# Two projections of values: 512 weight columns for four chunks of tokens in four PSUM banks, in place of 256 columns chunk by chunk

## The chip, the cores and the metric

The kernel runs on one core of one Trainium2 chip. The metric is the time of one execution on the device in microseconds (us), as the median of several runs. The profile shows one such execution.

## The reference

Two transformer blocks follow each other on 512 tokens of 1024 features. Each begins with a normalised and modulated input `u` and one wide projection of it, whose columns are then split into queries, keys, values and more:

```
z = u @ w_in[layer]
q_a, ..., q_b, k_b, v_b, m_a, m_b = jnp.split(z, split_at, axis=-1)          # first block
y_a = nsa_attention(q_a, ...) @ w_up_nsa;  y_b = stick_breaking_attention(q_b, k_b, v_b) @ w_up_sb
...
proj = hn @ w_in[l]
q_m, k_m, v_m, o_m, gates, q_a, k_a, v_a = jnp.split(proj, split_at, axis=-1)  # second block
h_m = mlstm_chunkwise(q_m, k_m, v_m, ...);  h_a = moba_attention(q_a, k_a, v_a)
```

The change touches how `v_b` of the first block and `v_a` of the second are computed. Both are a product of `u` (512 tokens by 1024) and 1024 by 512 weights.

## The kernel before, in words

Every fp32 product is made of three TensorE matmuls on operands split into a coarse and a fine part (`mm3`, L125, lines L127 to L129). `u` is held split, features on the partitions, as two tiles of 8 feature blocks by 512 tokens. Weights are loaded by `load` (L90) into one of two tiles `raw` of 1 MB, and split by `parts` (L104, L117: the coarse part on ACT, the fine part on DVE, 1024 columns at a time) into one of three pairs of tiles `w`.

Queries and keys are projected with the weights stationary and the 512 tokens moving (`project`, L816): each group of 128 output columns takes 24 matmuls of 512 columns, and PE's rows read `G<-u,w`. Values are wanted the other way round, tokens on the partitions. There `u` is stationary and the weights move (`project_rows`, L850): for each half of 256 columns it loads the weights, splits them in two calls, and goes through the four chunks of 128 tokens. A chunk takes 24 matmuls of 256 columns into one bank, and is copied out. PE's rows read `G<-w,u` with 128x256.

PSUM has eight banks. `ps` (L139) hands them out by tag: two banks `G`, three `S`, two `T`, one `O`. The banks of a tag go round in the order in which the program asks for them.

The order of instructions on each engine is set by a scheduler, which places work of later statements between that of earlier ones as far as data, banks and tiles allow. Two places matter here.

First block (`attention1`, L954): eight heads of one attention (`nsa_head`, L640) come first in the program. Their scores take the `S` banks (L679, L652), their transposes `T` (L522, L687), their output `O` (L691 once per head, as two matmuls; L530, L532). The projections of queries, keys and values of the other attention (L1024 to L1026, all in `G` banks) come behind the heads in the program. The scheduler lays their matmuls between the heads' on PE. So it does with the first groups of `take_m` (L1049), whose results can't leave their `G` banks before the heads end, since the tiles `mo` (L1042) lie where the heads' tiles lay. The heads of the second attention (`sb_head`, first matmul L743) start behind the last of the first eight.

Second block (`block2`, L1106): the projection of values (L1161) comes ahead of the eight heads `moba_head` (L1365, scores in `S` banks, L1383 and L1385). Two more projections, of 12 groups (L1165, L1166), and a third of values (L1167, `vm`, which stays on `project_rows`) are laid between these heads. Then come the four heads `mlstm_head` (L1299), each of which ends with a matmul L1353; the projection `mixa` (96 matmuls `G<-p,w`, L1188) is laid between them.

Of the kernel before, what the change touches and what calls it, by code (L numbers as in the profile page):

```python
# [14 lines left out]
AF = mybir.ActivationFunctionType  # L15
# [8 lines left out]
S, D = 512, 1024  # L24
# [48 lines left out]
class Kernel:  # L73
# [776 lines left out]
    def project_rows(self, u, name, c0, n, consume):  # L850

        for s in range(0, n, 256):
            w = self.load(self.w_cols(name, c0 + s, 256))
            w = [self.parts(w[:, 4 * i:4 * i + 4]) for i in range(2)]
            for t in range(4):
# [5 lines left out]
                if t % 2:  # L861
                    self.step()

    def block1(self, mods, dram, hp):


        nc = self.nc
        md = dram.tile([128, 16 * 512], F32, name="md")
        with ExitStack() as stack:
            with self.pool("b1n", "right") as wk:  # L870
                hr = wk.tile([128, 8, 512], F32, name="hr")
                with self.pool("b1a") as ap:
# [12 lines left out]
                    w = self.load(self.w_cols("w_in", 512, 256))  # L885
# [3 lines left out]
                u = [up.tile([128, 8, 512], F32R, name=f"u{i}") for i in range(2)]  # L889
# [64 lines left out]
    def attention1(self, u, md, first, dram):  # L954

        nc = self.nc
        kg = self.col("k_norm_g")
        gq = self.cp.tile([128, 1], F32, name="gq")
        nc.vector.tensor_scalar(gq, self.col("q_norm_g"), -0.125, None, op0=OP.mult)
        kd, vs = [], []  # L960
        sbq = self.sbq = ExitStack()
        with self.pool("nsap") as sp:

            places_a = Places([sbq.enter_context(self.pool("oa", "right"))] * 4, ("qn", "ob"), 1)
            qn = places_a.old[0]
            gates = sp.tile([128, 4, 4, 8], F32, name="gates")
            with self.pool("nsa0") as wk:

                def take_q(m, ps):
                    self.head_norm(ps, gq, qn[:, m], self.np)  # L970

                def take_k(b, ps):
                    kn = wk.tile([128, 512], F32, name="kn", bufs=2)
                    self.head_norm(ps, kg[:, b:b + 1], kn, wk)
                    t = [sp.tile([128, 2, 512], F32R, name=f"kd{b}{i}") for i in range(2)]
                    for g in range(2):
                        self.double(t[0][:, g], t[1][:, g], kn, 64 * g)
                    kd.append(t)

                def take_v(ps):  # L980
                    v = wk.tile([128, 512], F32, name="kn", bufs=2)
                    nc.scalar.activation(v, ps, AF.Copy)
                    t = sp.tile([128, 4, 2, 128], F32R, name=f"vs{len(vs)}")
                    self.values(t, v, wk)
                    vs.append(t)

                def take_kv(m, ps):
                    if m < 2:
                        self.compress_take(m, ps)
                    elif m in (2, 4):  # L990
                        take_k(m // 2, ps)
                    elif m in (3, 5):
                        take_v(ps)
                    else:
                        self.nsa_gates(ps, gates, wk)

                self.compress_start(wk)
                self.w_places = [(self.wp, 3)] * 3 + [(wk, 2)] * 2
                self.project(u, "w_in", 512, 896, take_kv, first=first, banks=[("G", 2)] * 2 + [("S", 3)] * 2)
                self.bias_bands(dram)  # L1000
                kdc, vsc = self.compress(sp, wk, kg[:, 0:1])
                self.project(u, "w_in", 0, 512, take_q)
                self.w_places = [(self.wp, 3)]

            sq = sbq.enter_context(self.pool("sbq", "right"))
            places = Places([sq] * 4, ("qT", "kT"))
            qT, kT = places.old
            vT = sq.tile([128, 4, 512], F32, name="vT")
            with self.pool("nsaw") as wk:

                heads = [self.nsa_head(h, qn, [[kd[b][i][:, h // 4] for i in range(2)] for b in range(2)], vs,
                                       kdc, vsc, gates, places_a.take, wk) for h in range(8)]
                self.in_turn(heads, 2)

            def keep(dst, scale):
                def f(m, ps):
                    nc.scalar.activation(dst[:, m], ps, AF.Copy, scale=scale)
                return f

            def take_vb(t, c0, ps):  # L1020
                nc.scalar.activation(vT[:, t, c0:c0 + 256], ps, AF.Copy)

            self.background = self.ada(0, [2, 3, 4])
            self.project(u, "w_in", 1304, 512, keep(qT, 0.125))  # L1024
            self.project(u, "w_in", 1816, 512, keep(kT, 1.0))
            self.project_rows(u, "w_in", 2328, 512, take_vb)  # L1026
        with self.pool("mo") as mw:
            self.sg = sbq.enter_context(self.pool("sg", "right"))
            with self.pool("sbw") as wk:

                self.in_turn([self.sb_head(h, qT, kT, vT, places.take, wk) for h in range(8)])


            self.kept = {}

            def take_m(first):
                def f(m, ps):
                    m += first
                    stay = m in (0, 1, 8)
                    t = self.sg.tile([128, 512], F32, name="sg", bufs=3) if stay else \  # L1040
                        mw.tile([128, 512], F32, name="mo", bufs=2)
                    nc.vector.tensor_copy(t, ps)  # L1042
                    if stay:
                        self.kept[m] = t
                    else:
                        nc.gpsimd.dma_start(md[:, m * 512:(m + 1) * 512], t)
                return f

            for m, n in ((2, 6), (10, 6), (0, 2), (8, 2)):  # L1049
                self.project(u, "w_in", 2840 + m * 128, n * 128, take_m(m))  # L1050
        return places_a.new, places.new
# [54 lines left out]
    def block2(self, h, u, up, mods, left, fp):  # L1106
# [8 lines left out]

        def rows_to(dst):
            def f(t, c0, ps):
                nc.vector.tensor_copy(dst[:, t, c0:c0 + 256], ps)
            return f

        vp = ExitStack()
        with up:
# [31 lines left out]
            with self.pool("vT", "right") as tp:  # L1154
                qT, kT = [Tiles([tp.tile([128, 1, 512], F32, name=f"{x}{j}") for j in range(4)], 1) for x in "qk"]
                vT = tp.tile([128, 4, 512], F32, name="vT")
                self.project(u, w_in, 2056, 512, keep(qT, -0.125), early=[None] * 3)
                with self.pool("mlr") as wk:
                    self.exps = [self.mlstm_rows(u, rows, acol, wk)]
                self.project(u, w_in, 2568, 512, keep(kT, 1.0))  # L1160
                self.project_rows(u, w_in, 3080, 512, rows_to(vT))  # L1161
                with self.pool("mbw") as wk:
                    for h8 in range(8):
                        self.moba_head(h8, qT, kT, vT, mixa, wk)
                    self.project(u, w_in, 1536, 512, keep(so, 0.5))  # L1165
                    self.project(u, w_in, 0, 1024, take_qk)  # L1166
                    self.project_rows(u, w_in, 1024, 512, rows_to(vm))  # L1167
# [797 lines left out]
```

## Time and profile before

| what | us |
|---|---|
| median of 3 runs (1805.99 to 1808.2) | 1807.76 |
| the profiled execution | 1805.68 |
| its span, first to last instruction | 1803.9 |
| TensorE (PE) busy | 1722.5 |
| VectorE (DVE) busy | 1397.3 |
| ScalarE (ACT) busy | 1143.0 |

Read the shares by stage, not as a whole. A busy PE is not a PE at its peak: matmuls are pipelined, a row lasts longer than the distance to the next one's start, and it is this distance that counts in a row of matmuls.

### The profile page before, as it was taken

Reading aid. Unit: us, or ns where it says so; the run is one execution under the profiler, and the core shown is the slowest. Engines: PE = TensorE matmul, PEld = TensorE weight load, DVE = VectorE, ACT = ScalarE, POOL = GpSimd, SP = SyncE. Lnnn points to the kernel's source line nnn. Section 1 sums busy time; section 2 is a strip of 40 time slices with the busy share of each in tenths; the row PEclk is TensorE's granted clock in tenths of the full one; section 3 lists DMA queues with packets and bytes.
Section 4 is the critical chain, followed back from the end, with each engine's and each line's share of the span. In section 5 each row is a group of like instructions: output and inputs, shape, how many; then the busy total and the mean of one; then the engine's idle time right before and its main releaser. Section 6 shows DMA issues by size and latency. Waiting matters only on the chain. (4 is left out here: it accounts for less than half of the span.)

```text
span 1803.9 us, 24830 instructions
## 1 busy us (share of the span) xinstructions
PE 1722.5 (95%) x8944; PEld 1414.6 (78%) x8944; DVE 1397.3 (77%) x2023; ACT 1143.0 (63%) x1805; POOL 474.6 (26%) x433
## 2 busy tenths in 40 slices
PE   5899999999999999999999999969999999999996
PEld 2678986787898888888979888757777777777775
DVE  4558888987788565657765867879999989999997
ACT  4356676665555343435555766558888878888886
POOL 2213424535133333333312410131212112121113
PEclk8999999999999999999999999979999999999998
DMA  8524213325655656564523215579999999999954
GB/s 324 166 92 129 83 59 116 102 87 164 197 180 165 208 182 201 177 207 149 165 71 94 63 56 175 212 232 345 356 360 362 348 313 385 376 365 364 371 204 168
DMA packets 233376, 377.71 MB, mean 209 GB/s; under 512 B 11817, under 2 KB 104613, under 8 KB 233248
## 3 DMA queue, kind: packets, MB, share of 16 engines
q1 hardware_dynamic: 221728, 345.60, 55.9%
q0 software_dynamic: 11520, 30.47, 5.5%
q8 instruction: 72, 1.18, 0.3%
q14 instruction: 56, 0.46, 0.1%
HBM read 366.64 MB, written 20.73 MB: 215 GB/s over the span
## 5 line engine op out<-in xcount | busy, mean ns | idle before, releaser
L117 ACT ACTIVATE w<-raw 128x1024 fp32r<-128x1024 f32 (+2 forms) x350 | 353.5, 1017 | 309.8 <-PE G L128 238.7
L117 DVE TENSOR_TENSOR w<-raw,w 128x1024 fp32r<-128x1024 f32 (+2 forms) x350 | 421.8, 1224 | 127.0 <-ACT w L117 123.6
L127 PE MATMUL G<-u,w 128*128 128x512 f32 (+1 forms) x688 | 267.5, 390 | 10.0 <-DVE cseq L599 6.6
L128 PE MATMUL G<-u,w 128*128 128x512 f32 (+1 forms) x688 | 266.2, 387 | 0.4 <-DVE u L229 0.4
L129 PE MATMUL G<-u,w 128*128 128x512 f32 (+1 forms) x688 | 265.6, 387 | 0.0
L127 PE MATMUL S<-w,x 128*128 128x512 f32 x504 | 198.3, 399 | 6.5 <-PEq L1791 3.5
L128 PE MATMUL S<-w,x 128*128 128x512 f32 x504 | 203.2, 403 | 0.0
L129 PE MATMUL S<-w,x 128*128 128x512 f32 x504 | 200.6, 398 | 0.1
L117 DVE TENSOR_TENSOR w<-rawa,w 128x1024 fp32r<-128x1024 f32 x122 | 149.7, 1259 | 19.4 <-ACT w L117 17.8
L127 PEld LDWEIGHTS G<-u,w 128*128 128x128 f32 x688 | 130.9, 191 | 35.6 <-issue 7.9
L128 PEld LDWEIGHTS G<-u,w 128*128 128x128 f32 x688 | 131.1, 191 | 27.2 <-DVE hr L894 1.1
L117 ACT ACTIVATE w<-rawa 128x1024 fp32r<-128x1024 f32 x122 | 127.8, 1060 | 36.9 <-PE S L129 22.4
L129 PEld LDWEIGHTS G<-u,w 128*128 128x128 f32 x688 | 130.8, 190 | 25.7 <-DVE w L117 0.9
L391 POOL TENSOR_TENSOR acc<-acc,araw 128x512 f32<-128x512 f32 x60 | 88.7, 1496 | 236.1 <-ACT araw L389 235.9
L127 PEld LDWEIGHTS S<-w,x 128*128 128x128 f32 x504 | 95.9, 190 | 29.9 <-issue 4.0
L129 PEld LDWEIGHTS S<-w,x 128*128 128x128 f32 x504 | 96.0, 190 | 22.3 <-POOL x L1646 0.9
L128 PEld LDWEIGHTS S<-w,x 128*128 128x128 f32 x504 | 96.0, 191 | 21.3
L128 PE MATMUL G<-hid,w 128*128 128x512 f32 (+1 forms) x320 | 111.1, 347 | 1.2 <-DVE hid L1083 1.2
L129 PE MATMUL G<-hid,w 128*128 128x512 f32 (+1 forms) x320 | 111.3, 348 | 0.0
L127 PE MATMUL G<-hid,w 128*128 128x512 f32 (+1 forms) x320 | 110.8, 347 | 0.0
L1646 POOL TENSOR_TENSOR x<-xg,x 128x512 fp32r<-128x512 f32 x32 | 47.6, 1488 | 229.2 <-ACT x L1645 229.2
L128 PE MATMUL G<-w,hh 128*128 128x512 f32 x248 | 100.9, 407 | 0.0
(635 smaller groups left out, 4028.4 us busy)
## 6 DMA issues: line engine op xcount, KB each, us to landing
raw<-in_mlp_w_dram SPq DMA_DIRECT2D x36, 1024.0 KB, 5.4
raw<-in_w_in_dram SPq DMA_DIRECT2D x33, 1024.0 KB, 5.4
raw<-in_w_expert_up_dram SPq DMA_DIRECT2D x28, 1024.0 KB, 10.5
raw<-in_w_expert_gate_dram SPq DMA_DIRECT2D x27, 1024.0 KB, 9.4
raw<-in_w_expert_down_dram SPq DMA_DIRECT2D x27, 1024.0 KB, 7.9
araw<-in_w_ada_dram SPq DMA_DIRECT2D x96, 256.0 KB, 3.7
rawa<-in_w_expert_gate_dram SPq DMA_DIRECT2D x21, 1024.0 KB, 10.6
rawa<-in_w_expert_up_dram SPq DMA_DIRECT2D x20, 1024.0 KB, 8.7
```

The costliest lines, as they stand in the source:

```text
L117: ins = nc.scalar.activation(r[0], v, AF.Copy), nc.vector.tensor_sub(r[1], v, r[0])
L127: first = nc.tensor.matmul(ps, lhs[0], rhs[0], start=start, stop=False)
L128: nc.tensor.matmul(ps, lhs[0], rhs[1], start=False, stop=False)
L129: self.behind = nc.tensor.matmul(ps, lhs[1], rhs[0], start=False, stop=stop)
L391: nc.gpsimd.tensor_add(x, x, raw)
L1646: nc.gpsimd.tensor_sub(x[1][:, s], y[:, s], x[0][:, s])
```

## The change

A new function `project_values` asks for four banks at once: two of tag `G` for the first two chunks of tokens, two of `S` for the others. It loads the weights as two halves of the 1024 features, each 4 blocks by all 512 columns, and splits each half in two calls of 2 blocks by 512 columns. For each such quarter it goes through the four chunks with six matmuls of 512 columns each. All four chunks are copied out behind the last quarter, 512 columns each, by ACT in the first block (`take_vb`) and by DVE in the second. There are 96 matmuls of 512 columns in place of 192 of 256, the same four splits of 1024 columns, two loads of 1 MB in runs of 2 KB in place of two in runs of 1 KB, four copies of 512 columns in place of eight of 256, and four calls of `step` as before. The third projection of values (L1167) stays as it is.

```diff
+    def project_values(self, u, name, c0, consume):
+        ps = [self.ps("G", 2) if t < 2 else self.ps("S", 3) for t in range(4)]
+        for half in range(2):
+            w = self.load(self.w_cols(name, c0, 512, 4 * half, 4))
+            for i in (0, 2):
+                v = self.parts(w[:, i:i + 2])
+                for t in range(4):
+                    for k in range(2):
+                        self.mm3(ps[t], [x[:, 4 * half + i + k, t * 128:(t + 1) * 128] for x in u],
+                                 [x[:, k] for x in v], half + i + k == 0, half == 1 and i + k == 3)
+                self.step()
+        for t in range(4):
+            consume(t, 0, ps[t])
...
-                nc.scalar.activation(vT[:, t, c0:c0 + 256], ps, AF.Copy)
+                nc.scalar.activation(vT[:, t], ps, AF.Copy)
...
-            self.project_rows(u, "w_in", 2328, 512, take_vb)
+            self.project_values(u, "w_in", 2328, take_vb)
...
-                nc.vector.tensor_copy(dst[:, t, c0:c0 + 256], ps)
+                nc.vector.tensor_copy(dst[:, t, c0:c0 + ps.shape[-1]], ps)
...
-                self.project_rows(u, w_in, 3080, 512, rows_to(vT))
+                self.project_values(u, w_in, 3080, rows_to(vT))
```

The scheduler's order changes with it, in the first block from the second of the eight heads to the start of its merge, and in the second block from the projection of values to the last `mlstm_head`; elsewhere the engines' rows are the same but for some ten instructions. Lines of the changed kernel behind the new function are 16 higher.

In the first block, the matmuls of projections that stand on PE's row between the heads' L691, counted in that row (wide: 512 columns, narrow: 256):

| stretch of PE's row | before | after |
|---|---|---|
| L691 of the 2nd head to the 3rd's | 61 narrow | 34 wide |
| 3rd to 4th | 79 narrow | none |
| 4th to 5th | 50 narrow, 14 wide | none |
| 5th to 6th | 34 wide | none |
| 6th to 7th | none | none |
| 7th to 8th | none | 58 wide |
| 8th to the last L532 | none | 49 wide |
| from there to the first L743 | 25 wide | 33 wide |

PE around the fifth head in the first block; first before, where `w_2818` and `w_2822` are weights of the values, then the same place after:

```order
L129 MATMUL G<-w_2822,u_409 128x256
L127 MATMUL G<-w_2822,u_408 128x256
L691 MATMUL O<-C,vsc 128x512
L530 MATMUL O<-P_1644,vs_621 128x512
L128 MATMUL G<-w_2823,u_408 128x256
L129 MATMUL G<-w_2822,u_409 128x256
L127 MATMUL G<-w_2818,u_408 128x256
```

```order
L679 MATMUL S<-kd_675,QS 128x384
L679 MATMUL S<-kd_676,QS 128x384
L522 MATMUL T<-ident,P 128x128 x4
L691 MATMUL O<-C,vsc 128x512
L530 MATMUL O<-P_1644,vs_621 128x512
L532 MATMUL O<-P_1645,vs_621 128x512
L530 MATMUL O<-P_1655,vs_621 128x384
```

The matmuls of the values have left this place, and the head's own follow each other. The chunks in `S` banks come behind the last score of the last head (L679), which is their place in the round of the three `S` banks. PE there, after:

```order
L679 MATMUL S<-kd_675,QS 128x512
L679 MATMUL S<-kd_676,QS 128x512
L127 MATMUL S<-w_2694,u_408 128x512
L128 MATMUL S<-w_2695,u_408 128x512
L129 MATMUL S<-w_2694,u_409 128x512
L127 MATMUL S<-w_2694,u_408 128x512
```

There the first three quarters of the weights, split long before, are used a second time; the fourth quarter is split only when one of the three pairs of tiles `w` comes free.

In the second block, PE at the start of the values; before, where the third score of the first `moba_head` stands ahead of the values' matmuls, then after:

```order
L1383 MATMUL S<-K_9224,QS 128x384
L1383 MATMUL S<-K_9225,QS 128x384
L1385 LDWEIGHTS ident_b
L1385 MATMUL S<-mask_at,ident_b 128x128
L127 MATMUL G<-w_8992,u_5452 128x256
L128 MATMUL G<-w_8993,u_5452 128x256
```

```order
L129 MATMUL S<-w_8978,u_5349 128x512
L1399 MATMUL S<-K_9016,QS 128x128
L1399 MATMUL S<-K_9017,QS 128x128
L1401 LDWEIGHTS ident_b
L1401 MATMUL S<-mask_at,ident_b 128x128
L127 MATMUL G<-u_5348,w_9660 128x512
```

After, the first score (L1399 is L1383 of before) stands behind all 96 matmuls of the values. Further on, the last matmul of the last `moba_head` stands 27 narrow matmuls ahead of the end of `vm`; before, 142. And of the 96 matmuls `G<-p,w`, 84 stand ahead of the first L1353 after, 36 before.

## Rows read from the trace of the kernel before

**Rows 1.** The page's head: the span, and PE's busy time.

```profile
span 1803.9 us, 24830 instructions
PE 1722.5 (95%) x8944; PEld 1414.6 (78%) x8944; DVE 1397.3 (77%) x2023; ACT 1143.0 (63%) x1805; POOL 474.6 (26%) x433
```

**Rows 2.** Stages: length, busy PE, PEld, DVE, ACT, POOL, clock, DMA, GB/s.

```profile
185.30:203.90 18.60, 18.60 (x140) 17.17 (x139) 17.34 (x53) 13.41 (x36) 7.12 (x10) 1.00 0.11 32
203.90:222.80 18.90, 18.90 (x146) 17.60 (x145) 15.22 (x45) 13.24 (x33) 6.94 (x11) 1.00 0.33 98
...
260.20:270.90 10.70, 10.28 (x67) 8.37 (x67) 10.12 (x39) 8.29 (x24) 3.72 (x6) 1.00 0.01 2
270.90:281.50 10.60, 8.35 (x45) 5.51 (x45) 8.90 (x26) 7.40 (x20) 3.98 (x6) 1.00 0.00 0
281.50:289.60 8.10, 7.83 (x45) 6.11 (x46) 3.63 (x8) 2.11 (x5) 0.00 (x0) 0.95 0.01 2
289.60:299.00 9.40, 8.39 (x28) 6.51 (x28) 9.27 (x12) 7.01 (x13) 7.25 (x6) 0.68 0.55 173
299.00:429.00 130.00, 125.14 (x662) 103.85 (x661) 112.16 (x166) 82.78 (x155) 58.93 (x51) 1.00 0.33 104
...
974.00:1068.00 94.00, 94.00 (x492) 77.84 (x491) 75.34 (x117) 59.39 (x127) 29.33 (x34) 1.00 0.25 77
1068.00:1094.40 26.40, 25.88 (x209) 25.42 (x208) 18.45 (x32) 21.58 (x41) 0.00 (x0) 1.00 0.14 49
```

**Rows 3.** Timeline, PE, L691 of four heads: start, length, engine, idle before.

```profile
185.27 1.12 PE L691 MATMUL O<-C,vsc 32*128 32x512 f32 x2
...
260.18 1.12 PE L691 MATMUL O<-C,vsc 32*128 32x512 f32 x2 [0.72 <-DVE sq L508]
270.88 1.12 PE L691 MATMUL O<-C,vsc 32*128 32x512 f32 x2 [0.40 <-DVE sq L508]
281.47 1.12 PE L691 MATMUL O<-C,vsc 32*128 32x512 f32 x2 [0.55 <-DVE sq L508]
```

**Rows 4.** Timeline, PE, second block: two neighbours of 256 columns, two of 512.

```profile
955.09 0.28 PE L128 MATMUL G<-w,u 128*128 128x256 f32 x1
955.21 0.28 PE L129 MATMUL G<-w,u 128*128 128x256 f32 x1
...
989.01 0.40 PE L128 MATMUL G<-u,w 128*128 128x512 f32 x1
989.24 0.39 PE L129 MATMUL G<-u,w 128*128 128x512 f32 x1
```

**Rows 5.** Timeline, PE, first block, from the last head's end.

```profile
289.62 0.41 PE L532 MATMUL O<-P,vs 128*128 128x256 f32 x1
291.04 0.80 PE L127 MATMUL G<-u,w 128*128 128x512 f32 x1 [1.01 <-DVE mo L1042]
...
292.06 0.63 PE L129 MATMUL G<-u,w 128*128 128x512 f32 x1
292.49 0.63 PE L127 MATMUL G<-u,w 128*128 128x512 f32 x1
...
298.97 0.61 PE L743 MATMUL T<-QS,K 128*128 128x512 f32 x2
```

**Rows 6.** Copies of values out of PSUM: ns min/median/max, first and last start.

```profile
L1021 ACT ACTIVATE vT<-G x8: 361/367/383, 194.7 to 238.5; 128x256 f32<-128x256 f32 x8
L1118 DVE COPY vT<-G x8: 406/424/425, 951.2 to 973.9; 128x256 f32<-128x256 f32 x8
```

**Rows 7.** The page's groups: DVE's part of the splits; busy us, mean ns, idle before.

```profile
L117 DVE TENSOR_TENSOR w<-raw,w 128x1024 fp32r<-128x1024 f32 (+2 forms) x350 | 421.8, 1224 | 127.0 <-ACT w L117 123.6
```

**Rows 8.** Timeline, PE, L1353 of the first three heads `mlstm_head`.

```profile
1107.73 1.02 PE L1353 MATMUL S<-sq,ones_h 128*128 128x512 f32 x2
1129.10 1.10 PE L1353 MATMUL S<-sq,ones_h 128*128 128x512 f32 x2
1141.15 1.02 PE L1353 MATMUL S<-sq,ones_h 128*128 128x512 f32 x2
```

## The prediction

> **What bounds the kernel now.** I read the page's head first: TensorE is busy for 1722.5 us of a span of 1803.9 us [rows 1], so the question is where PE still waits and what the change does to those waits. Next come the stages [rows 2], which show two kinds around the first change. While matmuls of projections lie between the heads, PE is busy throughout and a head takes 18.6 to 18.9 us. From 260.2 us on nothing lies between them, a head takes 10.7 and 10.6 us, DVE is busy for 10.12 us of the first 10.7, and PE waits a little for DVE ahead of each head's L691 [rows 2, 3]. So the filled heads are bound by PE, the bare ones by DVE. Last, the end of this stage [rows 5]: the last head ends at 290.0 us, PE waits 1.01 us for the copy that frees a `G` bank, and its matmuls then start 0.43 us apart, where a warm one of 512 columns has 0.23 [rows 4]. The granted clock in that stretch is 0.68 on average [rows 2], which means that part of it ran at 1.2 GHz, the rest at 2.4. The second heads' first matmul is at 298.97 us [rows 5], and from there PE is busy for 125.14 of 130 us [rows 2]: what is left to do then is nearly all paid for. In the second block PE is busy for 94.00 of 94.00 and 25.88 of 26.40 us [rows 2]; heads that run beside projections are hidden there.
>
> **The stream itself.** Neighbours of 256 columns start 0.12 us apart, those of 512 columns 0.23 us [rows 4]. A projection of values is 192 x 0.12 = 23.0 us before and 96 x 0.23 = 22.1 us after, 0.9 us less at each place. So wider matmuls alone give 1.8 us, 0.1%. A gain or a loss beyond that must come from where the work lies.
>
> The Trainium skill ("TensorE: Matmul & The Clock Gate", Back-to-back issue gap) gives 262 cycles for 256 columns and 518 for 512 at 2.4 GHz. By that, an estimate, the two projections save 0.5 us together in place of 1.8; the trace's distances are longer, and the sum goes by them.
>
> **First block, step by step.** The change does here only half of what it says: by the new order two chunks run early in `G` banks and two late in `S` banks, behind the heads' last score. I start at the second head's L691 at 185.27 us [rows 3], where both orders still agree, and count the projections' matmuls between heads by the table of the change.
> - Second to third head: 18.6 us before [rows 2] with 61 narrow matmuls (7.3 us); after, 34 wide ones (7.8 us). 19.1 us.
> - Third to seventh head: nothing between. Four times the bare 10.7 us [rows 2, 3] = 42.8 us. They were filled before, save the last.
> - Seventh to eighth: 58 wide matmuls, 13.3 us, beside a head's own work. How do the two add? In the filled head of 18.9 us [rows 2], 79 narrow matmuls are 9.5 us and leave 9.4 us for the head, 0.91 of the 10.28 us for which PE is busy in the bare one [rows 2]. The stage here has 8.35 us of busy PE [rows 2]; 0.91 of it is 7.6. Together 20.9 us.
> - From the eighth to the last L532: 49 wide, 11.3 us, and 0.91 of 7.83 us [rows 2] = 7.1. Together 18.4 us.
>
> The sum is 101.2 us, and the heads end at 286.5 us in place of 290.0: 3.5 us earlier. The second heads' preparation takes the 9.0 us from 290.0 to 298.97 again [rows 5]; in it PE has 33 wide matmuls (7.6 us) and the wait of 1.0 us for `mo`, 8.6 in all. The slow clock of [rows 5] should be gone, since PE streams up to there, but it lies under the 9.0 us and gives nothing by itself. Besides, by the first L743 PE has done 80 wide matmuls of `take_m` in place of 73, counted from the table: 7 x 0.23 = 1.6 us less for the stage behind, which PE bounds. **First block: -3.5 - 1.6 = -5.1 us.** Its 0.9 us of the stream are inside.
>
> The bounds: if PE's busy times of the last two steps are paid in full (8.35 and 7.83 us), the gain is 3.6 us. But busy rows overlap: one of 256 columns lasts 0.28 us where the next starts 0.12 us later [rows 4]. At that ratio of 0.43 the heads' share is 7.0 us in place of 14.7, and the gain 12.8. I take 0.91, from the only stage in which heads and projections are mixed.
>
> **What costs nothing.** The splits are the same four of 1024 columns. The fourth waits until a pair of `w` comes free, which is after 24 of the 36 wide matmuls that use the first three quarters again; 12 of them (2.8 us) and the head's own matmuls cover a split, of which DVE's part is 1.2 us [rows 7]. Behind it on DVE stand the next splits of `take_m`, on ACT these and the last head's; if the cover is gone, PE waits about that long, once. The two loads of 1 MB are the same bytes in longer runs; the DMA engines are busy for 0.11 to 0.33 of that stage [rows 2], and the first half is needed no earlier. Copies out of PSUM: eight at 0.367 us on ACT, eight at 0.424 us on DVE before [rows 6]; four of twice the width can't take more than those did, 2.9 and 3.4 us.
>
> **Second block.** The stream gives 0.9 us. The heads `moba_head` begin some 22 us into the values, where they began ahead of them, because two of the three `S` banks are held. PE has other work all that time, up to the end of `vm`, and the last head's last matmul still lies 27 narrow ones (3.2 us) ahead of it. The price is at the end: 84 of the 96 matmuls of `mixa` stand ahead of the first L1353, 36 before. So that one comes 48 x 0.23 = 11.0 us later, less the 0.9. The next stretch had the 60 others, and took 21.37 us; after it has 12, and I take the bare 12.05 us of the following one [rows 8]. 11.0 - 0.9 + 12.05 - 21.37 = +0.8 us. **Second block: +0.8 us**; between -0.9 (the heads hide it all) and +3 (each of three bare heads loses 1 us more).
>
> **The forecast.** -5.1 + 0.8 = -4.3 us. Against the profiled execution of 1805.68 us that is 1801.4. This execution is 2.1 us below the median of 1807.76; on the median's scale it is **1803.5 us**. By the bounds above the change lies between -13.7 and -0.6; the likely part is -8 to -1.
>
> **Rivals.**
> - *The displaced work isn't taken up.* The last two heads keep their bare 10.6 and 8.1 us, and the 13.3 and 11.3 us come on top. For it: DVE's order is fixed, and the bare stage waits for DVE [rows 3]. Against: filled heads show the two overlapping [rows 2]. 23.9 + 19.4 in place of 39.3 us: 4.0 us of the gain go, 1807.5.
> - *The copies come in a lump.* In the filled stages copies never held PE up, which was busy throughout [rows 2]. After, the banks come free together behind the last quarter, and the next group needs one. Laid open in full that is 2.9 and 3.4 us [rows 6]; I price half, 3.2 us: 1806.7. The Trainium skill ("Perfetto Trace Analysis", Optimizing Tensor Performance, Matmuls) asks that independent groups rotate through banks so that the copying of one overlaps the next one's matmuls, which speaks against opening four groups and closing them together; the same paragraph prefers larger matmuls.
> - *A moba head too late* (slower). If the eight heads run over the end of `vm` by one bare head, 12.05 us [rows 8] less the 3.2 us of cover: +8.9 us, 1812.4. It decides once they slip more than 3.2 us. Against: they have as long as PE's other work lasts, about 15 us each.
> - *The clock* (slower). It fell at the bare end: 0.95 in the stage to 289.6 us and 0.68 after it [rows 2], when PE had only the last head's scraps. The bare heads from 204 to 247 us could do the same. At 0.43 in place of 0.23 us per matmul [rows 4, 5], 9.4 us of PE work become 17.6, 6.9 more than 10.7, in each of four heads: +27.6, 1831; from one head on it decides the sign. Against: the clock was 1.00 in both bare heads from 260.2 to 281.5 us [rows 2].
> - *More*: the stage of the second heads starts with more done and loses its stalls: 1795 or less.
>
> **How the numbers follow.** Chances: forecast 0.62, work not taken up 0.11, copies 0.05, late head 0.05, clock 0.06, more 0.08, and 0.03 for reorderings that cost over 4 us. A measurement can tell about 0.2% from no change, 3.6 us. Of the forecast's own range three quarters lie beyond -3.6: 0.46; with *more*, faster is 0.54. Same: 0.16 of the forecast, 0.11 and 0.05, together 0.32. Slower: 0.14. The range leaves out the clock, the late head and the far end of *more*: 1796 to 1809.5.
>
> **What would show it.** Right: L691 some 10.7 us apart from about 204 to 247 us at clock 1.00; wide `S<-w,u` matmuls from about 249 us; the last head's end near 286 us; no matmul 0.43 us apart there; the first L743 near 295 us; the first L1353 some 10 us later and the fourth about a microsecond from where it was. Wrong: bare heads over 12 us or at a lower clock; PE idle ahead of the fourth quarter or of `take_m`'s first group; the last L691 later than 270 us; PE idle between 1068 and 1095 us.

## The result, and the profile after

The changed kernel is slower: 1822.35 us, the median of four runs (1814.35 to 1825.99), against 1806.88 us for the kernel before. The ratio is 1.0073, 95% interval 1.0056 to 1.009. A second set of five runs gave 1823.28 us and 1.0083 (1.007 to 1.0096). The forecast was 1803.5 us, with a range up to 1809.5.

The profiled execution of after is the fastest of the nine, 1814.35 us. The head of its page, which answers to [rows 1], shows PE as busy as before in a span 8.7 us longer: PE doesn't do more, it waits more.

```profile
span 1812.6 us, 24453 instructions
...
PE 1722.1 (95%) x8752; PEld 1403.2 (77%) x8752; DVE 1390.9 (77%) x2019; ACT 1141.2 (63%) x1801; POOL 466.1 (26%) x433
```

The stages of the first block, from the second head's L691 on, answer to [rows 2]. The columns are the same: stretch, length, busy PE, PEld, DVE, ACT, POOL, clock, DMA share, GB/s.

```profile
187.10:206.50 19.40, 19.40 (x112) 16.33 (x111) 15.78 (x48) 11.80 (x31) 6.47 (x9) 1.00 0.10 29
206.50:219.90 13.40, 11.11 (x68) 8.48 (x67) 13.06 (x47) 10.41 (x30) 6.33 (x11) 1.00 0.08 21
219.90:232.90 13.00, 10.80 (x66) 8.46 (x66) 11.60 (x40) 9.29 (x26) 4.31 (x9) 1.00 0.07 21
232.90:246.60 13.70, 11.15 (x67) 8.43 (x67) 13.21 (x43) 9.77 (x27) 5.52 (x9) 1.00 0.09 21
246.60:258.30 11.70, 10.64 (x67) 8.52 (x67) 9.94 (x35) 7.67 (x24) 2.76 (x5) 1.00 0.00 0
258.30:279.60 21.30, 20.89 (x103) 16.32 (x103) 12.80 (x28) 13.62 (x28) 3.90 (x6) 1.00 0.39 122
```

The four bare heads (second to fifth row) take 13.4, 13.0, 13.7 and 11.7 us, at full clock. That is 51.8 us where four times the 10.7 us of [rows 3] were forecast. The same rows of PE's timeline as in [rows 3] now read, with the wait ahead of each in brackets:

```profile
219.88 0.69 PE L691 MATMUL O<-C,vsc 32*128 32x512 f32 x1 [1.76 <-DVE sq L508]
232.95 0.69 PE L691 MATMUL O<-C,vsc 32*128 32x512 f32 x1 [2.04 <-DVE sq L508]
246.59 0.69 PE L691 MATMUL O<-C,vsc 32*128 32x512 f32 x1 [1.61 <-DVE sq L508]
```

Before it was 0.40 to 0.72 us. What PE waits for shows in the timeline of all engines ahead of the first of these (start, length, engine, line, operation):

```profile
216.16 0.36 PE L532 MATMUL O<-P,vs 128*128 128x256 f32 x1
...
217.16 0.44 DVE L694 TENSOR_SCALAR st<-st 128x4 f32<-128x4 f32 x1
217.32 0.57 ACT L507 ACTIVATE sq<-O 64x512 f32<-64x512 f32 x1
...
217.73 0.78 DVE L668 TENSOR_TENSOR ec<-ec,st 128x124 f32<-128x124 f32 x1
218.43 0.15 DVE L696 TENSOR_TENSOR st<-st,gates 128x4 f32<-128x4 f32 x1
218.62 0.49 DVE L709 TENSOR_SCALAR P<-P,st 128x512 f32<-128x512 f32 x1
...
219.14 0.69 DVE L508 TENSOR_TENSOR sq<-O,sq 64x512 f32<-64x512 f32 x1
```

The old head's last matmul into the one bank `O` ends at 216.52 us and ACT has read the bank by 217.89, but DVE's L508, which frees it, starts at 219.14. In DVE's fixed order the next head's preparation (L668, L696, L709) stands ahead of it. PE's L691, the next head's first matmul into `O`, waits for that.

This is also a part of why the price of 10.7 us was wrong. DVE's groups in the four bare heads of after together (line, operation, shapes, count, busy us, mean ns):

```profile
L694 DVE TENSOR_SCALAR st<-st 128x4 f32<-128x4 f32 x8 | 2.6, 326 | 0.0
...
L482 DVE TENSOR_TENSOR QS<-qn,QS 64x512 fp32r<-64x512 f32 x3 | 2.1, 686 | 0.1
L668 DVE TENSOR_TENSOR ec<-ec,st 128x124 f32<-128x124 f32 x4 | 2.0, 498 | 0.1
L696 DVE TENSOR_TENSOR st<-st,gates 128x4 f32<-128x4 f32 x8 | 1.7, 211 | 0.1
...
L170 DVE TENSOR_TENSOR ob<-sq,qn 128x512 fp32r<-128x512 f32 x2 | 1.4, 684 | 0.0
```

The full bare head of before has neither `QS` nor `ob`, and its small steps are shorter:

```profile
L694 DVE TENSOR_SCALAR st<-st 128x4 f32<-128x4 f32 x2 | 0.3, 156 | 0.0
L696 DVE TENSOR_TENSOR st<-st,gates 128x4 f32<-128x4 f32 x2 | 0.3, 154 | 0.0
...
L668 DVE TENSOR_TENSOR ec<-ec,st 128x124 f32<-128x124 f32 x1 | 0.3, 286 | 0.0
```

In the kernel before, the last `QS` for these heads and the `ob` of the last pair but one lie outside the only full bare head, which is 260.18 to 270.88 us. DVE's timeline of before:

```profile
249.67 0.69 DVE L482 TENSOR_TENSOR QS<-qn,QS 64x512 fp32r<-64x512 f32 x1
...
272.72 0.69 DVE L170 TENSOR_TENSOR ob<-sq,qn 128x512 fp32r<-128x512 f32 x1
```

So the head that gave the price is the one at the drain: the eighth head's queries had been stacked before it began, nothing came behind, and the split of a finished pair fell behind its end. DVE is busy for 10.12 us in it [rows 2] and for 11.95 on average in after's four. Of the 9.0 us that the four heads take beyond 42.8, `QS` and `ob` are 3.5 us of DVE's time. L694, L668 and L696 took some 2.7 us more than they would at the mean times of before (an estimate from the two lists); the last section shows beside what. The rest isn't taken apart. The last of the four, which is the same point of the sequence as before's, has neither `QS` nor `ob` and is the shortest, but it too took 11.7 us and not 10.7; why isn't shown.

### The profile page after: what moved, and what is told of

Same layout as the page of the kernel before. It is cut to its first block, busy times and chain, and to the rows that moved or that the text cites. A ratio compares the mean times of both kernels' runs of the same rounds, so it can differ in the third digit from the quotient of the medians.

```text
span 1812.6 us, 24453 instructions
## 1 busy us (share of the span) xinstructions
PE 1722.1 (95%) x8752; PEld 1403.2 (77%) x8752; DVE 1390.9 (77%) x2019; ACT 1141.2 (63%) x1801; POOL 466.1 (26%) x433
## 5 line engine op out<-in xcount | busy, mean ns | idle before, releaser
L127 PE MATMUL G<-u,w 128*128 128x512 f32 (+1 forms) x688 | 266.9, 389 | 10.7 <-DVE cseq L599 6.8
L128 PEld LDWEIGHTS S<-w,x 128*128 128x128 f32 x504 | 95.9, 190 | 21.3
```

What stands on the lines that cost most here:

```text
L127: first = nc.tensor.matmul(ps, lhs[0], rhs[0], start=start, stop=False)
L128: nc.tensor.matmul(ps, lhs[0], rhs[1], start=False, stop=False)
```

## The experiments

**Where the loss is: again, first_only, second_only.** The first is the changed kernel unaltered. The other two take the change back at one of its two places:

```diff
# first_only: the second place as before
-                self.project_values(u, w_in, 3080, rows_to(vT))
+                self.project_rows(u, w_in, 3080, 512, rows_to(vT))
# second_only: the first place as before
-            self.project_values(u, "w_in", 2328, take_vb)
+            self.project_rows(u, "w_in", 2328, 512, take_vb)
```

> The changed kernel again, to see where its own executions differ: the profiled one took 1814.35 us, the others 1820.45 to 1825.99. My theory is that the first block's bare heads (nothing of the projections between the third and the seventh L691) cost about 13.0 us each in place of 10.7, and that the rest of the spread is the granted clock, which can fall in such a stretch. Then the ratio is again 1.005 to 1.010, the four intervals from the third to the seventh L691 add up to 51 to 53 us where the clock is 1.00, and a slower execution shows a stretch at 1.2 GHz somewhere between 190 and 500 us that the first profile did not have. Rival: the spread is in the second block; then the last first-head L743 lies at about 307 us as in the first profile and the delay appears behind 974 us.

> The new function in the first block alone, the second block as before. Theory (the held G banks leave five heads bare at 13 us each): +6 to +14 us, a ratio of 1.004 to 1.008, the first L743 6 us later than before. Rival (the second block's late moba heads carry the loss): within 3 us of before, ratio 0.998 to 1.002.

> The new function in the second block alone, the first block as before. Theory (the second block is about neutral): the fourth L1353 0 to 3 us later than before, the whole time -1 to +2 us, ratio 0.9995 to 1.001. Rival (the second block carries the loss): +6 us or more, ratio over 1.003. The prediction had +0.8 us for this place.

Measured: first_only 1819.4 us, ratio 1.0066 (1.0048 to 1.0085), 11.3 us over before. second_only 1810.87 us, 1.0016 (1.0007 to 1.0024), 2.8 us over before. Both places lose, the first four times as much, and 14.1 us together is about what the change loses as a whole (15.2 us in these runs). The expectation for the second place was too small.

The profile of the unaltered kernel again, 1823.28 us, shows what the fastest execution did not:

```profile
219.90:233.00 13.10, 10.82 (x67) 8.47 (x67) 11.66 (x41) 9.32 (x27) 4.43 (x9) 1.00 0.07 21
233.00:250.50 17.50, 15.43 (x66) 12.05 (x66) 13.52 (x42) 9.98 (x27) 5.42 (x9) 0.70 0.06 16
250.50:264.50 14.00, 13.40 (x67) 10.52 (x67) 9.67 (x35) 7.89 (x24) 2.81 (x5) 0.76 0.00 0
264.50:287.30 22.80, 22.39 (x102) 17.61 (x102) 12.89 (x28) 13.76 (x28) 3.91 (x6) 0.93 0.37 116
```

The first two bare heads are as above. In the third, fourth and the head behind them the granted clock is 0.70, 0.76 and 0.93 on average, so that part of each ran at 1.2 GHz. They take 17.5, 14.0 and 22.8 us in place of 13.7, 11.7 and 21.3: 7.6 us of the 8.9 by which the two spans differ. The instructions, their order and the waits ahead of L691 (1.76, 2.04, 1.61 us) are the same in both executions.

**The price of a bare head: no_values.** The projection is left out (the values are then copies of the queries), and nothing of it has to be done later:

```diff
-            self.project_rows(u, "w_in", 2328, 512, take_vb)
+            for t in range(4):
+                nc.scalar.activation(vT[:, t], qT[:, t], AF.Copy)
```

> The kernel before with the first block's projection of values left out: vT is copied from the queries instead, so 192 matmuls of 256 columns (23.0 us), four splits and two loads are gone, and the third to the eighth heads are bare while nothing has to be done later in their place. It measures the price of a bare head by itself. Theory (13.0 us while the next head is prepared on DVE): third to seventh L691 52 us, seventh to eighth 10.7, the first L743 at about 287 us, 12 us earlier than before, so only half of the 23 us comes back. Rival, the prediction's price of 10.7 us per head: 42.8 us, the first L743 at about 278 us, 21 us earlier.

The stages of this kernel, third to seventh head:

```profile
210.40:225.20 14.80, 11.80 (x67) 8.58 (x67) 14.59 (x48) 11.40 (x31) 5.85 (x11) 1.00 0.13 37
225.20:238.20 13.00, 10.80 (x66) 8.44 (x66) 11.59 (x40) 9.29 (x26) 4.30 (x9) 1.00 0.08 21
238.20:252.90 14.70, 12.49 (x67) 9.73 (x67) 12.20 (x39) 9.17 (x26) 4.24 (x7) 0.88 0.07 19
252.90:264.60 11.70, 10.73 (x66) 8.46 (x66) 10.89 (x39) 8.76 (x26) 3.87 (x6) 1.00 0.01 1
```

54.2 us in place of 42.8, with the clock at 0.88 in the third: the bare head costs about 13 us without the change. The first L743 came at 291.4 us, 10.0 us earlier than before counted from the second head's L691, though 23.0 us of matmuls are gone. Where they stood before, the values' matmuls cost less than half of their length up to there, since they lay where PE would wait. The whole time was 1806.24 us, ratio 0.999 (0.9981 to 0.9999), which is only 1.9 us less. So most of the 10.0 us was lost again further on; in the profiled execution 2.9 of it between L743 and the first L463 of the following stage (165.9 us in place of 163.0). What loses it isn't shown.

**Width, banks or place: narrow_held, first_two, late.** narrow_held keeps the narrow matmuls and takes the banks; first_two keeps to the `G` banks and takes the width; late keeps both as before and moves the work by order alone. The code is shortened here.

```diff
# narrow_held, in project_rows at the first place
-                ps = self.ps("G", 2)
+                ps = self.ps("G", 2) if t < 2 else self.ps("S", 3)
# first_two: 512 columns, quarters q of the weights, chunks t
+        some(0, 0, v[0]); some(1, 0, v[0])          # some(t, q, v): six matmuls
+        v.append(quarter(3))
+        for t in range(2): for q in (1, 2, 3): some(t, q, v[q])
+        for t in (2, 3): for q in (1, 2, 3): some(t, q, v[q])
+        v[0] = quarter(0)
+        for t in (2, 3): some(t, 0, v[0])
# late: hold[i] is the L691 behind which the i-th group's first matmul is ordered
+            self.hold = [self.o_first[i] for i in [1, 1, 1, 6, 6, 6, 6, 6]]
             self.project_rows(u, "w_in", 2328, 512, take_vb)
```

> First block alone, 256 columns and the weights of before, but the chunks of tokens in banks G, G, S, S. It keeps the narrow matmuls and takes only the banks of the change. Theory (held G banks and late S banks leave heads bare, the width has no part in it): PE's row has nothing of the projections between the fifth and the seventh L691 and 12 narrow between the fourth and the fifth; bare heads take 12 to 14 us at full clock, and the time is +5 to +12 us over before, ratio 1.003 to 1.007. Rival (the width and its splits by quarters cost the time): within 3 us of before.

> First block alone, 512 columns, but two chunks at a time in the two G banks, the first quarter of the weights split a second time for the last two chunks (five splits in place of four, 2.2 us more of ACT and DVE); no S bank is held. It takes the width of the change without its banks. Theory: heads three to six stay filled (50, 44 and 48 wide matmuls between them), the time is that of before with 0.9 us less of stream and up to 2 us more of splits: -1 to +2 us, ratio 0.9995 to 1.001. Rival (width costs): +5 us or more as first_only.

> The kernel before with nothing changed but the order of PE's row: the first matmul of each of the last five groups of values (a chunk of tokens by 256 columns) is ordered behind the L691 of the seventh head. Width, banks G, copies and splits are those of before; only the place of the work is that of the changed kernel (72 narrow between the second and third L691, none up to the seventh, 106 narrow up to the eighth). Theory (what costs is that heads without projections wait for DVE, wherever their work went): third to seventh L691 51 to 54 us at full clock, +5 to +12 us over before, ratio 1.003 to 1.007. Rival (the wide matmuls, the four banks or the copies in a lump cost it): within 3 us of before.

late shows what the place does: 1816.94 us, ratio 1.0052 (1.0039 to 1.0065), with nothing changed but the place of the work. That is 9.6 us, of the 11.3 that first_only loses with width, banks and place together. Its bare heads (the line of L691 has another number there):

```profile
207.00:220.10 13.10, 10.71 (x67) 8.47 (x66) 11.03 (x41) 9.45 (x27) 3.53 (x7) 1.00 0.07 20
220.10:237.40 17.30, 15.15 (x67) 12.48 (x67) 12.32 (x42) 9.46 (x27) 5.17 (x10) 0.70 0.07 17
```

13.1 us where the clock is full, 17.3 where it is 0.70, as in the changed kernel. This is the execution of 1823.35 us; the other four took 1814.61 to 1818.86.

narrow_held gave 1812.94 us, 1.0031 (1.002 to 1.0042). Its bare heads take 12.3 to 14.5 us (two of them at a clock of 0.88 and 0.86), but up to the first L743 it needs 112.7 us from the second head's L691, where before needs 113.7. The loss came behind: from L743 to the first L463 of the following stage 170.0 us against 163.0. Nine matmuls of `take_m` (2.1 us) fewer were done at L743, and between the first two L774 PE had 13 wide matmuls and stood idle for 2.8 us of 8.0. So the size of the loss was forecast rightly, but it came at another place than expected. It looks as if work had moved away from a head that then waited, but the stage from L743 to L463 differs between kernels (168.3 us in late, 166.1 in first_two, 162.3 in after), and what sets it isn't shown.

first_two did not do what was expected: 1815.85 us, 1.0048 (1.0034 to 1.0062). The place has a part in it again; whether the width has one too in this block, this kernel doesn't tell. Wide groups of 50, 44 and 48 matmuls fill three heads with 10 to 11.5 us each, in place of four heads with 7 to 9.5, and two full bare heads are left, at 13.8 and 12.3 us, in place of one at 10.7:

```profile
230.30:252.10 21.80, 21.01 (x115) 17.39 (x114) 14.10 (x41) 12.91 (x30) 5.88 (x8) 1.00 0.29 91
252.10:265.90 13.80, 11.38 (x66) 8.58 (x66) 13.37 (x45) 9.90 (x28) 5.77 (x10) 1.00 0.08 20
265.90:278.20 12.30, 11.83 (x67) 9.64 (x67) 9.66 (x35) 8.13 (x23) 2.63 (x5) 0.86 0.00 0
```

**The second place: second_two, both_two.** The code of first_two, at the second place alone and at both. It keeps the heads ahead of the values, and 36 and 60 matmuls of `mixa` around the first L1353.

```diff
-                self.project_rows(u, w_in, 3080, 512, rows_to(vT))
+                self.project_two(u, w_in, 3080, rows_to(vT))
```

> As first_two, in both blocks. In the second block the heads begin ahead of the values again, as before, and 36 and 60 matmuls of mixa stand around the first L1353. Theory (the second block's loss of 2.8 us is the bare stretch between the first two L1353): the fourth L1353 within 1 us of before, the whole time -2 to +1 us, so that it is the only one of the wide kernels that might beat before. Rival (the wide values themselves cost in the second block): +2.5 us over first_two.

> The second block alone with 512 columns, two chunks at a time in the two G banks (five splits in place of four), the first block as before. The order of before is kept around the heads and around the L1353 (36 and 60 wide matmuls). Theory (second_only loses its 2.8 us in the bare stretch between the first two L1353, not by the width): the fourth L1353 within 1 us of before, the time -3 to 0 us (0.9 us of stream; both_two was 3.0 us below first_two), ratio 0.9985 to 1.000. Rival (the width costs there): +2 us or more.

second_two: 1807.56 us, 1.0003 (0.9994 to 1.0012), no difference. From the last L193 ahead of the values to the fourth L1353 it takes 251.2 us, before 251.9: 0.7 us less, near the 0.9 of the stream, with a fifth split to pay. second_only takes 254.1. So no cost of the width shows there where the order stays. both_two gave 1812.88 us, 1.0035 (1.0022 to 1.0049): 5.6 us over before where -2 to +1 was expected, with the loss of the first block in it. In second_only's timeline (its L1369 is L1353 of before):

```profile
1117.56 0.59 PE L1369 MATMUL S<-sq,ones_h 128*128 128x512 f32 x1
1132.62 0.70 PE L1369 MATMUL S<-sq,ones_h 128*128 128x512 f32 x1 [0.24 <-ACT sq L1362]
1143.91 0.70 PE L1369 MATMUL S<-sq,ones_h 128*128 128x512 f32 x1 [0.59 <-ACT sq L1362]
1154.23 0.59 PE L1369 MATMUL S<-sq,ones_h 128*128 128x512 f32 x1
```

The distances are 15.06, 11.29 and 10.32 us. Before they were 21.37 and 12.05 us [rows 8], and 10.0 to the fourth. The first L1353 comes 9.0 us later by the same start. 9.0 + 36.7 - 43.4 = +2.3 us, nearly the difference of 254.1 and 251.9.

**Is PE, DVE or the chain the bound: more_pe, more_dve, less_dve.**

```diff
# more_pe: ahead of the two matmuls of each score, in the third to seventh heads
+                for i in range(2 if 2 <= h <= 6 else 0):
+                    nc.tensor.matmul(ps[:, :n], QS[:, qb * 128:(qb + 1) * 128], kd[b][i][:, :n],
+                                     start=True, stop=True)
# more_dve: behind the scaling of row blocks 1 and 3, in the same heads
+                    nc.vector.tensor_sub(more, band[:, 0:128], band[:, 128:256])
# less_dve: the scaling of row block 3 left out, in the same heads
-                self.scale_rows(qb, P, sm)
+                if qb < 3 or not 2 <= h <= 6:
+                    self.scale_rows(qb, P, sm)
```

> The changed kernel with 16 matmuls more in each of the third to seventh heads, written ahead of the real scores into the same banks and overwritten by them: about 2.3 us more of PE per head (widths of 128 to 512, 320 on average, at 0.23 us per 512), 11.7 us in all. Theory (the changed kernel's executions of 1820 to 1826 us owe 7 to 9 us to half clock in bare heads whose PE is busy for 11 of 13 us): PE is busy throughout, the clock stays at 1.00 in all executions, the spread shrinks, and the median lies at 1815 to 1820 us, no higher than the changed kernel's 1823 although PE does more. Rival (the clock falls whatever PE does there, or the spread is from elsewhere): 1826 to 1835 us.

> The changed kernel with four more subtractions of 128x128 on DVE in each of the third to seventh heads (about 0.29 us each, 1.2 us per head), whose result nobody reads. If DVE's time sets the length of a bare head, the four intervals between the third and the seventh L691 grow from 51.8 us by 3.5 to 5 us at full clock. If it is only the chain of steps within a head, with room on DVE beside it, they grow by less than 1.5 us. In the evenly filled kernel the waits for DVE's L508 stayed although PE had 5.7 us of other work per head, which speaks for the chain.

> The changed kernel without DVE's scaling of the last row block of P (L709 of before, two of 128x512, 0.53 us each) in the third to seventh heads: that scaling is left out of what is computed. It takes 1.06 us per head off DVE and as much off the chain within the head. If DVE or the chain bounds a bare head, the four intervals shrink from 51.8 us by 2.5 to 4.5 us at full clock; if PE or POOL bounds it, by less than 1 us.

more_pe, in its first three bare heads:

```profile
210.80:223.90 13.10, 13.10 (x87) 11.47 (x86) 10.76 (x41) 9.01 (x25) 4.87 (x8) 1.00 0.07 20
223.90:236.70 12.80, 12.57 (x83) 10.73 (x82) 11.75 (x43) 9.82 (x28) 4.85 (x8) 1.00 0.09 22
236.70:250.40 13.70, 12.99 (x83) 10.88 (x82) 13.06 (x43) 10.38 (x29) 5.36 (x9) 1.00 0.08 21
```

16 matmuls more in each, and the heads are no longer than after's 13.4, 13.0 and 13.7 us. PE isn't their bound. The matmuls cost 4.5 us only in the stretch ahead, 23.9 us against 19.4, where PE was full already. The clock stayed at 1.00 in this execution. The median was 1820.8 us (1820.24 to 1826.28), ratio 1.0081 (1.0067 to 1.0095), just above what was expected if the clock held throughout; one execution of 1826.28 us is against it. That more PE work holds the clock is not shown.

more_dve didn't test what it was meant to. The scheduler laid 12 of its 20 subtractions ahead of the third L691. Only 8 ran between the third and the seventh; all of them first, then those in the four heads:

```profile
L701 DVE TENSOR_TENSOR more<-band x20: 257/288/1261, 168.9 to 235.3; 128x128 f32<-128x128 f32 x20
...
L701 DVE TENSOR_TENSOR more<-band 128x128 f32<-128x128 f32 x8 | 2.6, 320 | 0.0
```

The four heads took 14.5, 12.7, 14.1 and 10.7 us, 52.0 in all, where 2.6 us more of DVE as the bound called for 54.4. But the first, with four of the subtractions, grew by 1.2 us at a clock of 0.88, and the last, with none, shrank by 1.0. So this run doesn't tell DVE's time from the chain. less_dve shows its first bare head at full clock, and the fallen clock in the next:

```profile
206.70:219.00 12.30, 10.90 (x67) 8.41 (x66) 11.93 (x43) 10.51 (x30) 5.40 (x10) 1.00 0.08 23
219.00:236.20 17.20, 15.21 (x67) 12.46 (x67) 11.68 (x40) 9.47 (x27) 4.58 (x9) 0.70 0.06 16
```

12.3 us in place of 13.4: DVE's busy time is 1.1 us less, and so is the head, which either reading allows. Its other three ran at 0.66 to 0.70, so that their sum says nothing. Both are single executions. They show, with more_pe, that PE isn't the bound of a bare head and that DVE's steps are a part of it. Whether DVE's time or the chain of steps within a head sets its length stays open for these heads; before_less_dve and spread, below, speak for the chain with DVE's order in it.

**Looking for a better kernel: spread, spread_two, before_less_dve.**

```diff
# spread: as late, but evenly; spread_two: and second_two
+            self.hold = [self.o_first[i] for i in [1, 1, 2, 2, 3, 3, 4, 4]]     # values
+            self.hold = [self.o_first[i] for i in [5, 6]]                       # first groups of take_m
# before_less_dve: row block 3 on POOL too, in the last three heads
-        if qb < 3:
+        if qb < 3 or pool:
             self.nc.gpsimd.tensor_mul(x, x, s.to_broadcast(list(x.shape)))
```

> The kernel before with the same work laid evenly, again by order alone: 48 narrow matmuls (5.7 us) in each of the four stretches from the second to the sixth L691, then one group of take_m (24 wide, 5.5 us) in each of the two up to the eighth, where before had up to 79 narrow and then two bare heads. Theory (each head waits for DVE unless PE has some 3 us of other work; more than that is simply added): no idle PE up to the eighth L691, -3 to 0 us, ratio 0.998 to 1.000. Rival (the place of the work doesn't matter as long as no long bare stretch comes): within 1 us of before, with no difference in PE's idle time.

> spread in the first block and second_two in the second, the version that should beat both kernels if the two theories hold: the sum of the two, -6 to 0 us, ratio 0.997 to 1.000. If the two places don't add up, it lies at the higher of the two.

> The kernel before with that scaling on POOL in place of DVE in the last three heads, which are bare or nearly so. POOL is busy for 3.7 to 4.0 us of their 10.7. Theory (DVE bounds them): 0.5 to 1 us less for each of two bare heads, -2 to 0 us in all, ratio 0.999 to 1.000. Rival (the chain bounds them, and POOL's slower multiplication lengthens it): 0 to +3 us.

All three missed. spread took 1816.36 us, 1.0054 (1.0039 to 1.0069); spread_two 1815.91 us, 1.0054 (1.004 to 1.0068). Two heads of spread, and its waits of PE for L508 (us, times, longest) between the third and the eighth head:

```profile
203.60:220.80 17.20, 15.96 (x115) 13.96 (x115) 14.12 (x42) 12.91 (x32) 4.23 (x7) 1.00 0.22 62
220.80:237.90 17.10, 17.10 (x115) 15.54 (x115) 11.54 (x42) 9.88 (x29) 4.84 (x8) 0.90 0.20 63
```

```profile
PE O L691 <- DVE sq L508: 3.0, 5, 0.8
```

From the second to the eighth L691 it takes 102.5 us, before 96.2, with as much other work in between. With 5.7 us of it beside each head PE still waits, 5.8 us in all against 3.4, and in two heads the clock averages 0.90 and 0.91, which is another 3.3 us of full clock. Those two make 5.7 of the 6.3 us. So the simple rule behind the expectation, that some 3 us of other work fill a head, is wrong. Heads of before with 7.3 and 9.5 us of it ran without a pause [rows 2], but one with 7.8 us (34 wide, fifth to sixth L691) waited 0.72 us [rows 3], and of spread's four with 5.7 us three paused; the one that didn't ran at a clock of 0.90. In the first head shown PE is idle for 1.24 us although DVE is busy for only 14.12 of 17.20: that speaks for a wait in DVE's order rather than a full DVE.

before_less_dve gave 1808.31 us, 1.0009 (1.0 to 1.0018). In its profiled execution the first bare head ran at a clock of 0.66 and took 15.1 us, so that head can meet a fallen clock in the order of before too. The second ran at full clock:

```profile
277.70:288.20 10.50, 8.61 (x45) 5.56 (x45) 7.72 (x23) 7.26 (x20) 5.96 (x8) 1.00 0.00 0
```

DVE is busy for 7.72 us in place of 8.90, and the head takes 10.5 us in place of 10.6, so how full DVE is doesn't set this one's length. No version here beats the kernel before.

## Why the prediction was wrong

- **The step that failed is "Third to seventh head: four times the bare 10.7 us".** It measured 51.8 us in the best execution, 9.0 more than forecast. The prediction said rightly that the bare heads were bound by DVE's side and not by PE, and read the price from the one full bare head of before. That one stands at the drain and lacks the next head's preparation. no_values and late measured 13.0 and 13.1 us for a bare head at full clock without any of the change's matmuls (14.8 for the first of no_values). The missing preparation accounts for 3.5 of the 9.0 us, small steps of DVE that lasted longer for some 2.7; the rest is open. Nothing else is needed to turn the sign: -5.1 us for the first block becomes +3.9, and +5.8 were measured from the second head's L691 to the last L193 ahead of the second place.
- **The neighbouring steps held.** Second to third head 19.4 us (forecast 19.1), seventh to eighth 21.3 (20.9), from there to the first L743 27.4 (18.4 + 9.0). The rivals "the displaced work isn't taken up" and "copies in a lump" thus didn't happen. Of the 1.6 us that the next stage was to save, 0.7 came: from L743 to the first L463 162.3 us in place of 163.0.
- **The clock rival was underrated.** It had a chance of 0.06 and a price of 6.9 us per head. Per head the price was too high: again lost 3.8 us in one head and 2.3 in the next. The clock didn't fall in the bare heads of the fastest execution. In the other eight its mean over the span is 0.974 to 0.977 against 0.981, and the one of them that was profiled shows 7.6 us lost to it, half of the 15.2 us that the change costs in those runs. The argument against it, a clock of 1.00 in two bare heads [rows 2], came from one execution and from heads that are shorter and fewer.
- **The second block was mis-sized, +2.2 us in place of +0.8**, within its bounds of -0.9 to +3, by second_only's profile. The first L1353 came 9.0 us later, not 10.1. The next stretch was priced as bare, 12.05 us, but 12 wide matmuls stood in it: 2.8 us, which lie on top (12.05 + 2.8 = 14.85 in all, measured 15.06). In the two profiled executions of the changed kernel the block cost 3.0 and 4.7 us; there the clock averaged 0.90 and 0.86 between the first two L1353, which the prediction had at full clock. Of the 8.7 us between the two profiled spans, 5.8 and 3.0 are these two places; 1.9 more lie ahead of the second head's L691, and behind the fourth L1353 after took 2.0 less, neither of which is explained. The rival "a moba head too late" didn't happen: in second_only PE is busy for 30.50 us of the 30.5 around the end of `vm`.
- **The stream's 0.9 us per place is real**: second_two shows 0.7 of it where the order stays as it was. It is too little to be seen in the whole time.

What stays open is what decides in which execution the clock falls, what sets the length of the stage from L743 to L463, and whether L508 ahead of the next head's steps in DVE's order would shorten a bare head; that was not tried.

## What to carry to other kernels

Price a repeated step by one from the middle of its row: before using the last one, count its instructions against another's and see whether the preparation for a successor is missing. Work laid between waiting steps costs less than its length where it lies (up to L743, 10.0 of 23.0 us by no_values) and may cost most of it where it is moved to (10.7 of 13.3 us between the seventh and the eighth L691), so a change of banks can be first of all a change of place. And a clock of 1.00 in one profiled execution says little for stretches in which PE often pauses: look at several executions' clocks before giving such a rival a small chance.

## What the runs showed of the hardware

The granted clock differs between executions of one program in one stretch. With the same instructions and the same waits of 0.5 to 2.0 us ahead of each L691, the head from 233 us on had 1.00 in one execution of the changed kernel and 0.70 in another. The Trainium skill ("TensorE: Matmul & The Clock Gate", A second HAM failure mode: psum-queue depth-cycling) tells that short pauses of PE between groups of matmuls, if they are frequent, can make the clock swing between its two levels. The executions agree with that; why it happens in some and not in others, no run here shows.

Small steps of DVE took up to five times as long beside POOL (GpSimd): L694 0.79 us in the second bare head, where 0.16 is usual. In the first bare head L668 takes 0.78 us and ends at 218.51 us, where L707's last multiplication on POOL ends at 218.36. POOL's row (three in a row) and another L668, in the third bare head, are:

```profile
216.34 2.02 POOL L707 TENSOR_TENSOR P<-P,st 128x128 f32<-128x128 f32 x3 [3.50 <-DVE st L664]
```

```profile
244.31 0.28 DVE L668 TENSOR_TENSOR ec<-ec,st 128x124 f32<-128x124 f32 x1
```

The second one began just ahead of the POOL instruction that ran beside it (244.33 us), and took its 0.28 us. The Trainium skill ("SBUF — State Buffer", Who interferes with whom) says that a DVE instruction with two inputs in SBUF and a GpSimd instruction that reads SBUF exclude each other, and that the one issued later waits. L668 has two such inputs, and these rows agree with it. In L668's case that is half a microsecond just ahead of L508. L694, which has only one, was lengthened too. All seven steps of L665, L668, L694 and L696 that were lengthened in the first three bare heads ended 0.02 to 0.15 us behind the end of a POOL multiplication, while the reciprocals L666 and L695 kept their usual 0.16 to 0.18 us beside POOL.
